# A two-layer decoder step on one core: in the memory layer, weight splits queued behind keys, values and a group norm bias, one head's key transposes in another PSUM pool, and the last head's tail reordered

## The chip, the core and the metric

The kernel runs on one core of a Trainium2 chip. The metric is the device time of one execution in microseconds (us); the runs shown are medians. Engines are named as the profile names them: PE (TensorE matmuls), PEld (its weight loads), DVE (VectorE), ACT (ScalarE), POOL (GpSimd), SP (SyncE, which issues the DMAs).

## The reference: what is computed

One inference step of a two-layer decoder trunk on 320 tokens: 256 of a new prompt and 8 sequences of 8 sampled tokens. Layer 0 mixes tokens with a gated MLP, layer 1 with an mLSTM matrix memory; each is followed by a gated feed-forward layer with a short convolution. The change lies in layer 1, the memory layer. Cut to what matters there:

```
def mlstm_mixer(x, conv_buf, C0, n0, m0, w_in, conv_w, conv_b, b_i, b_f, gn_g, w_out):
    p = x @ w_in                                  # q, k, v, o of 8 heads, gates i, f
    qk, new_buf = causal_dwconv(qk_pre, conv_buf, conv_w, conv_b)
    qk = silu(qk)                                 # q and k: 128 per head; v and o: 256 per head
    h, C, n, m = mlstm_chunkwise(q, k, v32, ig, lf, C0, n0, m0)
    #   scores sc = (q k^T) * w_intra;  num = w_inter * (q C0) + sc v
    #   h = num / max(|den|, exp(-m));  C_new = decay * C0 + (k * g)^T v
    mu, var = mean(h), var(h)                     # group norm over a head's 256
    hn = (h - mu) * rsqrt(var + EPS) * gn_g
    y = (sigmoid(o_pre) * hn) @ w_out
```

All products with weights are float32; every operand is split into a high and a low part, and three matmuls are issued for each pair (high by high, high by low, low by high).

## The kernel before

**Weights.** Every weight block of 128 output columns is read from HBM in chunks of up to 8 tiles of 128x128 (`raw`, four buffers). `weights()` writes the list of all chunks in the order of use (`wq`). `prefetch(n, m)` issues the loads of the first n chunks on SP and the splits of the first m: a cast on ACT (`wh`, L136) and a subtraction on DVE (`wl`, L137), each pair in one of three buffers. `take()` hands out the next chunk, and first has the load of four chunks ahead and the split of one chunk ahead written. `block(kt, rhs)` multiplies a whole block into one of three PSUM banks of the pool `psm` (tile `pm`, 24 matmuls for 8 tiles); all smaller products share the five banks of the pool `psa`.

**Order.** The program is written engine by engine through a scheduling layer: PE's instructions are pinned to the order of the text (`pin`), those of DVE, ACT and POOL may be moved past each other by the layer, and `issue_after(ins)` holds what a block of text writes behind `ins` on that instruction's engine. `behind_split()` uses it to hold the statistics behind the last split. Once built, each engine runs its own list strictly in order.

**The memory layer's loop.** `layer_b` goes over the 8 heads; in the loop body h is the current head, and work of head h-1 is finished inside it. For a head there are six blocks of weights, here called q, k, v0, v1, o0 and o1. Per turn, on PE: block q; `close(h-1)` (the numerators `num` in `numer`, the prompt's new state `pCp` in `state_prompt`); blocks k, v0, v1; `scores(h)` (tiles `pMb`, `psc`); `k_nat(h)` (three transposes of keys into a bank `pk`); `finish(h-1)` (six transposes `phn` of the normed rows `hn`); block o0; `v_nat(h)` (six transposes of values, `pv`); block o1; `hand_over(h)` (`inter`: products of the query with the old state into `num`; `state_sample`: the update `pcs` of the 8 sampled states, in four banks of `psa`; `state_out` adds it to `C` and stores it). For h = 1, `close(0)` and `hand_over(0)` come later, among blocks k, v0 and v1, and `finish(0)` comes after block o0.

**Where the other engines stand.** `qk_epi` turns a block q or k into `qs`: a scaled copy (`bpad`), a convolution of one ACT (`bcv`, L695) and three DVE instructions (L697), a tanh on ACT (`bth`), two products on DVE (`qs`), then the high part on ACT (`qh`, `kh`) and the low part on DVE (`qhl`, `khl`, L281). The third score matmul reads `khl`. `stats(h)` reads `num` on DVE, takes an inverse root on POOL (`sl`, L854), forms the bias `nb` on DVE (L856), and writes `hn` in three ACT instructions (L858), which are the last readers of the three `num` banks. The last turn, h = 7, and what follows the loop mix in blocks of the output weights (`b_wo`): `begin(m)` opens output block m with the rows that are ready, the loop over m at the end closes it with the remaining rows.

Of the kernel before, what the change touches and what calls it, by code (L numbers as in the profile page):

```python
# [10 lines left out]
F32 = mybir.dt.float32  # L11
F32R = mybir.dt.float32r
AF = mybir.ActivationFunctionType
# [3 lines left out]
P = 128  # L17
# [21 lines left out]
class Net:  # L39
# [23 lines left out]
    def weights(self):  # L63
# [32 lines left out]
        add(I["b_wo"], 2, 6, k0=8)  # L96
        add(I["b_wo"], 0, 4, k0=12)
        for b in (1, 2):
            add(I["b_wo"], b, 2, k0=14)
        for b in range(3, KD):  # L100
# [8 lines left out]
    def prefetch(self, n, m):  # L109

        nc = self.nc
        while len(self.loaded) < min(n, len(self.wq)):
            w, b, k0, kn = self.wq[len(self.loaded)]
            raw = self.wraw.tile([P, 8, P], F32, tag="raw", name="raw")
            if w is self.I["a_wv"]:
                kn *= 4
                nc.sync.dma_start(raw[:, :kn, :], w[b, :, 4 * k0:4 * k0 + kn, :])
            else:
                nc.sync.dma_start(raw[:, :kn, :], w[b, :, k0:k0 + kn, :])
            self.loaded.append(raw)  # L120
# [33 lines left out]
    def chunk(self, ps, rhs, first, last):  # L154
        (wh, wl), kn = self.take()
        for k in range(kn):
# [122 lines left out]
    def split(self, yh, yl, y):  # L279
        self.nc.scalar.copy(yh, y)  # L280
        self.nc.vector.tensor_tensor(yl, y, yh.bitcast(F32), op=SUB)  # L281

# [273 lines left out]
    def layer_b(self):  # L556
# [5 lines left out]
        with ExitStack() as ctx:  # L562
# [120 lines left out]
            def qk_epi(h, j, ps):  # L683
# [18 lines left out]
                tv, c_ = [x[:, 256:].rearrange("p (b e) -> p b e", e=11)[:, :, 3:11] for x in (th, cv)]  # L702
                nc.vector.scalar_tensor_tensor(seg(qs[:, TP:T]), tv, 1.0, c_, op0=ADD, op1=MULT)
                nm = "kh" if j else "qh"
# [6 lines left out]
                self.split(hh, ll, qs[:, :n])  # L711
                s["qk"[j]] = (qs, hh, ll)
# [44 lines left out]
            def v_nat(h):  # L757
# [6 lines left out]
                for t in (2, 0, 1):  # L764
                    dst = dsts[t]
                    sc = self.rc[:, t:t + 1] if t < 2 else self.rc2
                    nc.scalar.activation(vh[:, t, :DV], dst[:, :DV], AF.Copy, scale=sc)
                    nc.vector.scalar_tensor_tensor(vl[:, t, :DV], dst[:, :DV], sc, vh[:, t, :DV].bitcast(F32), op0=MULT, op1=SUB)

            def k_nat(h):  # L770
                s = S[h]
                ks = s["k"][0]
                pk = self.psa.tile([P, 512], F32, tag="pa", name="pk")
                for t in range(3):
# [43 lines left out]
            def state_out(h, g):  # L818
                s = S[h]
                dec, C0, pcs = s["P"][2], s["C"][g], s["pcs"][g]  # L820
                for u in range(2):
                    b = 2 * g + u
                    nc.scalar.activation(C0[:, u, :DV], C0[:, u, :DV], AF.Copy, scale=dec[:, b:b + 1])
                nc.vector.tensor_tensor(C0[:, :, :DV], C0[:, :, :DV], pcs.rearrange("p (u v) -> p u v", u=2), op=ADD)
                nc.sync.dma_start(O["Cs"][h, :, 2 * g:2 * g + 2, :], C0[:, :, :DV])
# [15 lines left out]
            def stats(h):  # L841
# [13 lines left out]
                nb = hp.tile([P, 3], F32, tag="nb", name="nb", bufs=1)  # L855
                nc.vector.scalar_tensor_tensor(nb, mv[:, :, 0], -1.0, sl, op0=MULT, op1=MULT)  # L856
                for t in range(3):
# [90 lines left out]
            for h in range(1, NH):  # L948
                last = h == NH - 1
                ps = second if h == 1 else blk()  # L950
                if h > 1:
                    close(h - 1)
# [15 lines left out]
                early(h, 2)  # L968
                ps = blk()
                if h == 1:  # L970
                    with self.behind_split():
                        stats(0)
                v_epi(h, 1, ps)
                scores(h)
                k_nat(h)
                if h > 1:
                    finish(h - 1)
                early(h, 3)
                if last:
                    begin(0)  # L980
                else:
                    o_epi(h, 0, blk())
                if h == 1:
                    finish(0)
                early(h, 4)
                v_nat(h)
                if not last:
                    o_epi(h, 1, blk())
                    hand_over(h)
# [12 lines left out]
            finish(h)  # L1002
            state_sample(h)
            for g in range(4):
                state_out(h, g)
            begin(2)
            nc.gpsimd.tensor_tensor(nS, n0, decs, op=MULT)
            nc.gpsimd.tensor_tensor(nS, nS, nPS[:, :, 2:], op=ADD)
            nc.sync.dma_start(O["nP"], nPS[:, :, 0])
            nc.sync.dma_start(O["nS"], nS)  # L1010
            for m in range(KD):
                ps = part.get(m)
                if ps is None:
                    ps = self.block(8, lambda k: Y[8 + k])
                else:
                    self.chunk(ps, lambda k: Y[done[m] + k], False, True)
                self.residual_norm(m, ps, V_FFN + 8)


# [143 lines left out]
```

## Time and profile before

| | us |
|---|---|
| median of 3 runs (964.19 to 965.17) | 964.74 |
| the profiled execution's own time | 964.48 |
| its span, first to last instruction | 962.8 |
| PE busy | 948.8 (99%) |
| DVE busy | 672.1 (70%) |
| ACT busy | 520.4 (54%) |
| POOL busy | 79.5 (8%) |

The granted TensorE clock is 0.996 over the span. Matmuls are pipelined and their ends are modelled, so PE's gaps are read best as the distance from one matmul's start to the next's: in a block of weights it is 0.15 us, and 24 matmuls take 3.52 us. Timeline rows read: start in us, duration in us, engine, line, operation, out<-in, shapes, count, and in brackets the engine's idle time before the row and what ended it.

The memory layer lies between 425 and 721 us of the span; of its heads, h = 3 takes 514 to 543 us, and the output blocks after the loop start at 692 us.

### The profile page before, as it was taken

Reading aid. Unit: us, or ns where it says so; the run is one execution under the profiler, and the core shown is the slowest. Engines: PE = TensorE matmul, PEld = TensorE weight load, DVE = VectorE, ACT = ScalarE, POOL = GpSimd, SP = SyncE. Lnnn points to the kernel's source line nnn. Section 1 sums busy time; section 2 is a strip of 40 time slices with the busy share of each in tenths; the row PEclk is TensorE's granted clock in tenths of the full one; section 3 lists DMA queues with packets and bytes.
Section 4 is the critical chain, followed back from the end, with each engine's and each line's share of the span. In section 5 each row is a group of like instructions: output and inputs, shape, how many; then the busy total and the mean of one; then the engine's idle time right before and its main releaser. Section 6 shows DMA issues by size and latency. Waiting matters only on the chain.

```text
span 962.8 us, 17155 instructions
## 1 busy us (share of the span) xinstructions
PE 948.8 (99%) x6529; PEld 923.7 (96%) x6529; DVE 672.1 (70%) x1229; ACT 520.4 (54%) x948; POOL 79.5 (8%) x251
## 2 busy tenths in 40 slices
PE   9999999999999999999999999999999999999996
PEld 7779999999999999999899999999999999999996
DVE  5758985577777764549888877676787777775442
ACT  6557444355544543347777776575665555444332
POOL 2200000010000000013211001010101000000000
PEclk9999999999999999999999999999999999999998
DMA  7836344444444454456566555634473444445531
GB/s 252 237 131 183 125 139 150 148 142 154 153 141 152 145 153 151 148 196 209 192 203 203 178 174 187 209 127 152 87 247 136 154 154 150 139 147 153 155 121 55
DMA packets 57560, 154.71 MB, mean 161 GB/s; under 512 B 7734, under 2 KB 19382, under 8 KB 57478
## 3 DMA queue, kind: packets, MB, share of 16 engines
q1 hardware_dynamic: 57478, 153.62, 49.2%
q8 instruction: 51, 0.84, 0.3%
q14 instruction: 31, 0.25, 0.1%
HBM read 141.66 MB, written 11.94 MB: 160 GB/s over the span
## 4 chain that ended last, share of the span: by engine, by line
PE 85%; issue 10%; DVE 2%; DMA 1%; ACT 0%; SPq 0%; POOL 0%; DVEq 0%; POOLq 0%; ACTq 0%
PE pm L48 74%; PE pv L48 3%; PE num L48 2%; DMA raw<-in_a_wv 1%; PE pvs L48 1%; PE pmix L48 1%; DVE wl L137 1%; PE pCp L48 1%; PE psc L48 1%; PE pcs L48 1%; PE pv L51 1%; PE phn L51 0%; PE pk L51 0%; PE pc L48 0%; PE pg L48 0%
## 5 line engine op out<-in xcount | busy, mean ns | idle before, releaser
L136 ACT CAST wh<-raw 128x1024 fp32r<-128x1024 f32 (+3 forms) x255 | 257.9, 1012 | 306.5 <-PE pm L48 167.1
L137 DVE TENSOR_TENSOR wl<-raw,wh 128x1024 fp32r<-128x1024 f32 (+3 forms) x255 | 301.2, 1181 | 137.8 <-ACT wh L136 135.0
L48 PE MATMUL pm<-xh,wh 128*128 128x320 f32 x1216 | 379.7, 312 | 0.0
L48 PE MATMUL pm<-xh,wl 128*128 128x320 f32 x1216 | 376.0, 309 | 0.0
L48 PE MATMUL pm<-xl,wh 128*128 128x320 f32 x1216 | 375.8, 309 | 0.0
L48 PEld LDWEIGHTS pm<-xh,wh 128*128 128x128 f32 x1216 | 228.5, 188 | 0.7
L48 PEld LDWEIGHTS pm<-xl,wh 128*128 128x128 f32 x1216 | 228.5, 188 | 0.2
L48 PEld LDWEIGHTS pm<-xh,wl 128*128 128x128 f32 x1216 | 228.3, 188 | 0.0
L48 PE MATMUL pm<-yh_f,wh 128*128 128x320 f32 x352 | 109.2, 310 | 0.0
L48 PE MATMUL pm<-yh_f,wl 128*128 128x320 f32 x352 | 108.7, 309 | 0.0
L48 PE MATMUL pm<-yl_f,wh 128*128 128x320 f32 x352 | 108.7, 309 | 0.0
L48 PEld LDWEIGHTS pm<-yl_f,wh 128*128 128x128 f32 x352 | 66.1, 188 | 0.0
L48 PEld LDWEIGHTS pm<-yh_f,wh 128*128 128x128 f32 x352 | 66.1, 188 | 0.0
L48 PEld LDWEIGHTS pm<-yh_f,wl 128*128 128x128 f32 x352 | 66.1, 188 | 0.0
L478 DVE SCALAR_TENSOR_TENSOR fcv<-fpad,vecs,fcv 128x336 f32<-128x336 f32 x88 | 49.5, 565 | 2.2 <-ACT fcv L476 0.7
L272 DVE TENSOR_TENSOR xT<-pm,xT 128x320 f32<-128x320 f32 x40 | 19.6, 490 | 42.8 <-PE pm L48 42.8
L48 PE MATMUL pm<-yhb,wh 128*128 128x320 f32 x128 | 40.2, 314 | 0.0
L48 PE MATMUL pm<-yhb,wl 128*128 128x320 f32 x128 | 39.5, 309 | 0.5 <-DVE wl L137 0.5
L48 PE MATMUL pm<-yh_a,wh 128*128 128x320 f32 x128 | 39.6, 309 | 0.0
L48 PE MATMUL pm<-yl_a,wh 128*128 128x320 f32 x128 | 39.5, 309 | 0.0
L48 PE MATMUL pm<-yh_a,wl 128*128 128x320 f32 x128 | 39.5, 309 | 0.0
L48 PE MATMUL pm<-ylb,wh 128*128 128x320 f32 x128 | 39.5, 309 | 0.0
(254 smaller groups left out, 1273.7 us busy)
## 6 DMA issues: line engine op xcount, KB each, us to landing
raw<-in_f_up SPq DMA_DIRECT2D x88, 512.0 KB, 3.3
raw<-in_b_win SPq DMA_DIRECT2D x48, 512.0 KB, 4.4
raw<-in_f_dn SPq DMA_DIRECT2D x32, 448.0 KB, 3.2
C<-in_C SPq DMA_DIRECT2D x32, 258.0 KB, 4.9
raw<-in_a_win SPq DMA_DIRECT2D x16, 512.0 KB, 3.3
raw<-in_a_wo SPq DMA_DIRECT2D x16, 512.0 KB, 3.6
raw<-in_f_dn SPq DMA_DIRECT2D x16, 512.0 KB, 3.5
out_Cs<-C SPq DMA_DIRECT2D x32, 256.0 KB, 4.2
```

The lines of the kernel that those rows point to most:

```text
L48: self.pin(self.nc.tensor.matmul(out, lhsT, rhs, start=start, stop=stop))
L51: self.pin(self.nc.tensor.transpose(out, in_, ident))
L136: self.last_split = nc.scalar.copy(wh[:, :kn, :], raw[:, :kn, :])
L137: self.last_low = nc.vector.tensor_tensor(wl[:, :kn, :], raw[:, :kn, :], wh[:, :kn, :].bitcast(F32), op=SUB)
L272: self.nc.vector.tensor_tensor(x, ps[:, :T], x, op=ADD)
L478: nc.vector.scalar_tensor_tensor(cv, pd[:, i:i + NC], self.vec(w + i * KF), cv, op0=MULT, op1=ADD)
```

## The change

Four things, all in the memory layer:

1. **Splits held back or pulled ahead.** `split`, the convolution's last product, the state's decay, the group norm bias and the value splits are kept by name, and a new helper `behind(...)` holds what is written in its block behind them. For h > 1, the split of the chunk of block o0 is written behind `khl`, and what block v1's `take` writes behind `kh` and `khl`; block o1's `take` is behind the values' halves. `nb` of head h-1 is behind the product `qs` of block k of head h (the name `conv` holds the later of q's and k's). `stats(h-1)` is no longer held behind a split. For h = 1 and h = 2 there are three places more of the kind.
2. **Key transposes of the second head.** For h = 1, `k_nat` writes into a bank of `psm` instead of `psa`.
3. **Order in h = 1.** `finish(0)` comes after `v_nat(1)`, no longer ahead of it.
4. **The tail.** The last rows of output blocks 0, 1 and 2 (4, 2 and 2 tiles) are loaded by three DMAs into one `raw` tile and split at once, not as three chunks. `state_sample(7)` and `state_out(7)` come after output block 2, no longer ahead of `begin(2)`.

```
-        add(I["b_wo"], 0, 4, k0=12)
-        for b in (1, 2):
-            add(I["b_wo"], b, 2, k0=14)
+        q.append((I["b_wo"], ((0, 12, 4), (1, 14, 2), (2, 14, 2)), 0, 8))
...
     def split(self, yh, yl, y):
-        self.nc.scalar.copy(yh, y)
-        self.nc.vector.tensor_tensor(yl, y, yh.bitcast(F32), op=SUB)
+        return (self.nc.scalar.copy(yh, y),
+                self.nc.vector.tensor_tensor(yl, y, yh.bitcast(F32), op=SUB))
+
+    @contextmanager
+    def behind(self, *done):
+
+        with ExitStack() as held:
+            for i in done:
+                held.enter_context(self.tc.issue_after(i.ins))
+            yield
...
-                nc.vector.scalar_tensor_tensor(nb, mv[:, :, 0], -1.0, sl, op0=MULT, op1=MULT)
+                with self.behind(*([S[h + 1]["conv"]] if h + 1 < NH else [])):
+                    s["nb"] = nc.vector.scalar_tensor_tensor(nb, mv[:, :, 0], -1.0, sl, op0=MULT, op1=MULT)
...
-                ps = second if h == 1 else blk()
-                if h > 1:
+                if h == 1:
+                    ps = second
+                else:
+                    with self.behind(*([S[1]["decayed"]] if h == 2 else [])):
+                        ps = blk()
                     close(h - 1)
...
-                ps = blk()
                 if h == 1:
-                    with self.behind_split():
-                        stats(0)
+                    stats(0)
+                else:
+                    with self.behind(S[h]["halves"][1]):
+                        self.prefetch(0, self.used + 2)
+                with self.behind(*S[h]["halves"]):
+                    ps = blk()
                 v_epi(h, 1, ps)
                 scores(h)
-                k_nat(h)
+                k_nat(h, self.psm.tile([P, 512], F32, tag="pm", name="pk") if h == 1 else None)
                 if h > 1:
                     finish(h - 1)
...
-                    o_epi(h, 0, blk())
+                    with self.behind(*([S[0]["nb"]] if h == 1 else [])):
+                        ps = blk()
+                    o_epi(h, 0, ps)
+                if h > 1:
+                    early(h, 4)
+                v_nat(h)
                 if h == 1:
                     finish(0)
-                early(h, 4)
-                v_nat(h)
                 if not last:
-                    o_epi(h, 1, blk())
+                    with self.behind(S[h]["vh"], S[h]["vl"]):
+                        ps = blk()
+                    o_epi(h, 1, ps)
                     hand_over(h)
...
             finish(h)
-            state_sample(h)
-            for g in range(4):
-                state_out(h, g)
             begin(2)
...
+            (wh, wl), k = self.take()
             for m in range(KD):
...
-                    self.chunk(ps, lambda k: Y[done[m] + k], False, True)
+                    n = 16 - done[m]
+                    self.rows(ps, wh, wl, n, lambda k: Y[done[m] + k], False, True)
+                    wh, wl = wh[:, n:, :], wl[:, n:, :]
                 self.residual_norm(m, ps, V_FFN + 8)
+                if m == 2:
+                    state_sample(h)
+                    for g in range(4):
+                        state_out(h, g)
```

`rows` is the loop of `chunk` with the chunk handed in. Up to the memory layer the lists of all engines are the same, and PE's list differs in two places only: in h = 1 the six `pv` stand ahead of the six `phn`, and in the tail the sixteen `pcs` stand 42 matmuls later. On the other engines the built lists show more than the text does. Three places follow.

DVE in the turn h = 3, from the last `rd` of the statistics to the query's `Qz`; before, `wl_6006`, `wl_6099` and `wl_6148` are the low parts of the chunks for o0, o1 and the next head's q, and after, o0's is `wl_6003`.

```order
L852 TENSOR_SCALAR rd_5988<-rd_5988,mv0_4913 128x3
L137 TENSOR_TENSOR wl_6006<-raw_5804,wh_6005 128x1024
L697 TENSOR_SCALAR bcv_5923<-bpad1_4500,vecs_79,bcv_5923 128x344
L856 TENSOR_SCALAR nb_5994<-mv0_4913,sl_5992 128x3
L697 TENSOR_SCALAR bcv_5923<-bpad1_4500,vecs_79,bcv_5923 128x344 x2
L701 TENSOR_SCALAR qs_5930<-bth_5928,bcv_5923 128x256
L703 TENSOR_SCALAR qs_5930<-bth_5928,bcv_5923 128x64
L137 TENSOR_TENSOR wl_6099<-raw_5888,wh_6098 128x1024
L281 TENSOR_TENSOR khl_5934<-qs_5930,kh_5933 128x128
L137 TENSOR_TENSOR wl_6148<-raw_5948,wh_6147 128x1024
L733 TENSOR_SCALAR Qz_4904<-qs_5880,pMb_6036 128x8x8
```

The same place on DVE after:

```order
L860 TENSOR_SCALAR rd_5988<-rd_5988,mv0_4913 128x3
L705 TENSOR_SCALAR bcv_5923<-bpad1_4500,vecs_79,bcv_5923 128x344 x3
L709 TENSOR_SCALAR qs_5930<-bth_5928,bcv_5923 128x256
L711 TENSOR_SCALAR qs_5930<-bth_5928,bcv_5923 128x64
L865 TENSOR_SCALAR nb_5994<-mv0_4913,sl_5992 128x3
L281 TENSOR_TENSOR khl_5934<-qs_5930,kh_5933 128x128
L134 TENSOR_TENSOR wl_6003<-raw_5804,wh_6002 128x1024
L134 TENSOR_TENSOR wl_6099<-raw_5888,wh_6098 128x1024
L741 TENSOR_SCALAR Qz_4904<-qs_5880,pMb_6036 128x8x8
```

No split stands ahead of `khl` any more, `nb` has moved behind `qs`, and the split of the next head's q has left this stretch: it stands after the three `vl`. The turns h = 2 to 6 read alike; in h = 5 and 6, with a block of `b_wo` among them, three splits stand behind `khl`.

ACT in the turn h = 3, from the cast of o0's chunk on, before:

```order
L136 COPY wh_6005<-raw_5804 128x1024
L695 ACTIVATE bcv_5923<-bpad1_4500,vecs_79 128x344
L858 ACTIVATE hn_4906<-num_5842,nb_5994,sl_5992 128x256
L858 ACTIVATE hn_4906<-num_5843,nb_5994,sl_5992 128x256
L858 ACTIVATE hn_4906<-num_5766,nb_5994,sl_5992 128x256
L699 ACTIVATE bth_5928<-bcv_5923 128x344
L716 COPY vTb_5999<-pm_5947 128x256
L717 COPY vTb_5999<-pm_5947 128x128
L136 COPY wh_6098<-raw_5888 128x1024
L710 COPY ks_5935<-qs_5930 128x128
L280 COPY kh_5933<-qs_5930 128x128
```

And after:

```order
L133 COPY wh_6002<-raw_5804 128x1024
L703 ACTIVATE bcv_5923<-bpad1_4500,vecs_79 128x344
L133 COPY wh_6098<-raw_5888 128x1024
L707 ACTIVATE bth_5928<-bcv_5923 128x344
L724 COPY vTb_5999<-pm_5947 128x256
L725 COPY vTb_5999<-pm_5947 128x128
L280 COPY kh_5933<-qs_5930 128x128
L718 COPY ks_5935<-qs_5930 128x128
L867 ACTIVATE hn_4906<-num_5842,nb_5994,sl_5992 128x256
L867 ACTIVATE hn_4906<-num_5843,nb_5994,sl_5992 128x256
L867 ACTIVATE hn_4906<-num_5766,nb_5994,sl_5992 128x256
```

The cast of o1's chunk (`wh_6098`) now stands ahead of the tanh instead of behind the value copies, and the three `hn` stand behind the key's halves instead of ahead of the tanh.

DVE in the tail, from the second of the three small splits (output blocks 0, 1 and 2) to the split of output block 3 (`wl_8315`), before:

```order
L137 TENSOR_TENSOR wl_8274<-raw_8085,wh_8273 128x256
L891 TENSOR_SCALAR y_b_8202<-th_o_8186,phn_8198 128x320
L894 TENSOR_SCALAR ylb_8189<-y_b_8194,gnh_4487,yhb_8188 128x320
L824 TENSOR_TENSOR C0_7847<-C0_7847,pcs_8206 128x2x256
L894 TENSOR_SCALAR ylb_8189<-y_b_8202,gnh_4487,yhb_8188 128x320
L824 TENSOR_TENSOR C0_7849<-C0_7849,pcs_8207 128x2x256
L824 TENSOR_TENSOR C0_7851<-C0_7851,pcs_8208 128x2x256
L824 TENSOR_TENSOR C0_7853<-C0_7853,pcs_8209 128x2x256
L137 TENSOR_TENSOR wl_8297<-raw_8154,wh_8296 128x256
L272 TENSOR_TENSOR xT_76<-pm_8003,xT_76 128x320
L272 TENSOR_TENSOR xT_76<-pm_8037,xT_76 128x320
L137 TENSOR_TENSOR wl_8315<-raw_8243,wh_8314 128x1024
```

And after, where `wl_8240` is output block 3's and `wl_8324` output block 4's:

```order
L134 TENSOR_TENSOR wl_8240<-raw_8087,wh_8239 128x1024
L903 TENSOR_SCALAR ylb_8191<-y_b_8196,gnh_4487,yhb_8190 128x320
L900 TENSOR_SCALAR y_b_8204<-th_o_8188,phn_8200 128x320
L903 TENSOR_SCALAR ylb_8191<-y_b_8204,gnh_4487,yhb_8190 128x320
L134 TENSOR_TENSOR wl_8324<-raw_8156,wh_8323 128x1024
L272 TENSOR_TENSOR xT_76<-pm_8003,xT_76 128x320
L272 TENSOR_TENSOR xT_76<-pm_8037,xT_76 128x320
```

The split of output block 3 has moved from behind the two residual sums `xT` to ahead of the last head's `ylb`, and the four `C` have left this stretch.

More of the change, by code (lines that the diff above doesn't have):

```diff
@@ L114, in prefetch @@
             raw = self.wraw.tile([P, 8, P], F32, tag="raw", name="raw")
[L115 to L119, printed above, removed]
+            e, i = 4 if w is self.I["a_wv"] else 1, 0
+            for b, k0, kn in b if isinstance(b, tuple) else ((b, e * k0, e * kn),):
+                nc.sync.dma_start(raw[:, i:i + kn, :], w[b, :, k0:k0 + kn, :])
+                i += kn
             self.loaded.append(raw)
@@ L155, in chunk, with rows @@
         (wh, wl), kn = self.take()
+        self.rows(ps, wh, wl, kn, rhs, first, last)
+    def rows(self, ps, wh, wl, kn, rhs, first, last):
         for k in range(kn):
@@ L702, in qk_epi @@
                 tv, c_ = [x[:, 256:].rearrange("p (b e) -> p b e", e=11)[:, :, 3:11] for x in (th, cv)]
-                nc.vector.scalar_tensor_tensor(seg(qs[:, TP:T]), tv, 1.0, c_, op0=ADD, op1=MULT)
+                s["conv"] = nc.vector.scalar_tensor_tensor(seg(qs[:, TP:T]), tv, 1.0, c_, op0=ADD, op1=MULT)
                 nm = "kh" if j else "qh"
@@ L710, in qk_epi @@
                     nc.scalar.copy(spread(s["ks"]), twice(qs[:, TP:T]))
-                self.split(hh, ll, qs[:, :n])
+                s["halves"] = self.split(hh, ll, qs[:, :n])
                 s["qk"[j]] = (qs, hh, ll)
@@ L766, in v_nat, with k_nat @@
                     sc = self.rc[:, t:t + 1] if t < 2 else self.rc2
-                    nc.scalar.activation(vh[:, t, :DV], dst[:, :DV], AF.Copy, scale=sc)
-                    nc.vector.scalar_tensor_tensor(vl[:, t, :DV], dst[:, :DV], sc, vh[:, t, :DV].bitcast(F32), op0=MULT, op1=SUB)
-            def k_nat(h):
+                    s["vh"] = nc.scalar.activation(vh[:, t, :DV], dst[:, :DV], AF.Copy, scale=sc)
+                    s["vl"] = nc.vector.scalar_tensor_tensor(vl[:, t, :DV], dst[:, :DV], sc, vh[:, t, :DV].bitcast(F32), op0=MULT, op1=SUB)
+            def k_nat(h, bank=None):
                 s = S[h]
                 ks = s["k"][0]
-                pk = self.psa.tile([P, 512], F32, tag="pa", name="pk")
+                pk = bank or self.psa.tile([P, 512], F32, tag="pa", name="pk")
                 for t in range(3):
@@ L822, in state_out @@
                     b = 2 * g + u
-                    nc.scalar.activation(C0[:, u, :DV], C0[:, u, :DV], AF.Copy, scale=dec[:, b:b + 1])
+                    s["decayed"] = nc.scalar.activation(C0[:, u, :DV], C0[:, u, :DV], AF.Copy, scale=dec[:, b:b + 1])
                 nc.vector.tensor_tensor(C0[:, :, :DV], C0[:, :, :DV], pcs.rearrange("p (u v) -> p u v", u=2), op=ADD)
```

## The prediction

> **What bounds the kernel now.** I read the busy shares on the page first, then a table of two stretches, then PE's waits, and last the timeline around each wait.
>
> ```profile
> span 962.8 us, 17155 instructions
> PE 948.8 (99%) x6529; PEld 923.7 (96%) x6529; DVE 672.1 (70%) x1229; ACT 520.4 (54%) x948; POOL 79.5 (8%) x251
> 502.10:673.10 171.00, 168.52 (x1283) 162.89 (x1282) 134.42 (x288) 112.55 (x258) 16.84 (x42) 1.00 0.53 175
> 703.40:953.00 249.60, 249.60 (x1708) 249.39 (x1707) 161.05 (x258) 115.00 (x184) 13.99 (x70) 1.00 0.44 142
> ```
>
> In the two stretches (length; busy time of PE, PEld, DVE, ACT, POOL; clock) the clock is 1.00. In the last feed-forward layer PE has no gap at all; in the memory layer's heads 2.5 us of 171 are gaps. So PE is the bound, nothing here changes its matmuls, and the change can only win gaps back or open new ones. PE's waits name them:
>
> ```profile
> PE psc L48 <- DVE khl L281: 2.5, 5, 0.5
> PE pk L51 <- ACT hn L858: 1.5, 1, 1.5
> ```
>
> Five times the third score matmul waits for `khl`, once the key transposes wait for `hn`. Here is the former in h = 3, and below it the same pair of matmuls in h = 1, where nothing is waited for.
>
> ```profile
> 530.66 0.28 PE L48 MATMUL psc<-qh,kh 128*128 128x256 f32 x1
> 530.78 0.28 PE L48 MATMUL psc<-qhl,kh 128*128 128x256 f32 x1
> 531.55 0.39 PE L48 MATMUL psc<-qh,khl 128*128 128x256 f32 x1 [0.49 <-DVE khl L281]
> ...
> 532.50 0.38 PE L51 MATMUL phn<-ident,hn 128*128 128x128 f32 x2
> 472.25 0.28 PE L48 MATMUL psc<-qhl,kh 128*128 128x256 f32 x1
> 472.36 0.28 PE L48 MATMUL psc<-qh,khl 128*128 128x256 f32 x1
> ```
>
> From start to start the wait costs 0.77 − 0.11 = 0.66 us, more than the 0.49 in brackets, since the pipeline drains and fills again. All terms below are taken from starts.
>
> **Part 1: the splits, h = 3 to 6.** DVE and ACT of h = 3 before:
>
> ```profile
> 528.70 0.42 DVE L701 SCALAR_TENSOR_TENSOR qs<-bth,bcv 128x256 f32<-128x256 f32 x1 [0.82 <-ACT bth L699]
> 530.07 1.23 DVE L137 TENSOR_TENSOR wl<-raw,wh 128x1024 fp32r<-128x1024 f32 x1 [0.81 <-ACT wh L136]
> 531.22 0.28 DVE L281 TENSOR_TENSOR khl<-qs,kh 128x128 fp32r<-128x128 f32 x1
> 526.81 1.48 ACT L858 ACTIVATE hn<-num,nb,sl 128x256 f32<-128x256 f32 x3 [1.57 <-DVE nb L856]
> 528.17 0.49 ACT L699 ACTIVATE bth<-bcv 128x344 f32<-128x344 f32 x1
> 528.97 1.07 ACT L136 CAST wh<-raw 128x1024 fp32r<-128x1024 f32 x1
> 530.11 0.33 ACT L280 CAST kh<-qs 128x128 fp32r<-128x128 f32 x1
> 519.97 10.69 PE pm L48 x72
> ```
>
> `khl` needs only `kh`, done at 530.44, but a whole split (1.23) stands ahead of it on DVE, whose cast (1.07) stands ahead of `kh` on ACT. Afterwards the split of block o0 is behind `khl`. In exchange the cast for o1 is pulled ahead of `bth`, and it needs the buffer that block v0 has read. The last row, of the chain, gives three blocks (k, v0, v1) from 519.97 to 530.66, 3.56 each; v0 ends at about 527.1. The cast then ends at 527.1 + 1.07 = 528.2, and `bth` at 528.2 + 0.49 = 528.7, against 528.66 before. So `bth` loses nothing, as `hn` (1.48) has left the place ahead of it. From `bth` on `qs`, `kh` and `khl` follow each other: the two `qs` take 0.60 (0.42 and the narrow one), `kh` 0.33 and `khl` 0.28, with hardly a gap 1.2: `khl` is there at about 529.9. Its turn on PE is 530.78 + 0.11 = 530.89. Margin 0.9 to 1.0: the wait goes.
>
> What is late next: `hn`, now behind `kh` on ACT and behind `nb`, which is behind `qs` on DVE. `kh` ends at about 529.6; with the narrow copy behind it `hn`'s 1.48 end at about 531.2. Without the psc wait `phn`'s turn comes at 532.50 − 0.66 = 531.84. Margin 0.6, the thinnest of this change. The split for o0, whose cast stands early on ACT, now follows `khl` on DVE and is needed first by o0's third matmul:
>
> ```profile
> 533.45 0.31 PE L48 MATMUL pm<-xh,wl 128*128 128x320 f32 x1
> ```
>
> at 533.45 − 0.66 = 532.79; an estimate from 529.9 + 1.23 is 531.1, 1.7 early. The split for o1 comes 1.23 behind it, at 532.3, a whole block (3.56) ahead of its use. The next head's q, whose split stood here, goes behind the values' halves; its turn comes only after o1, the `inter` and the update. SP's loads keep their order, four chunks ahead of use, and POOL's list hardly changes; if a load came late, its whole chunk would wait, which the run would show as `pm` waiting. I take the full 0.66 in each of h = 3 to 6: **−2.6**. In h = 2 I take nothing: there the DVE work that h = 1 leaves over reaches into blocks q and k (bounds: −0.66 and, if one split of 1.23 less the 0.49 waited now comes on top, +0.75).
>
> **Part 2 and 3: h = 1.**
>
> ```profile
> 472.71 0.33 PE L48 MATMUL psc<-qs,ks 128*128 128x64 f32 x2
> 474.58 0.44 PE L51 MATMUL pk<-ident,qs 128*128 128x128 f32 x2 [1.54 <-ACT hn L858]
> 473.76 0.16 DVE L856 SCALAR_TENSOR_TENSOR nb<-mv,sl 128x3 f32<-128x3 f32 x1 [0.98 <-POOL sl L854]
> 484.23 0.47 DVE L768 SCALAR_TENSOR_TENSOR vl<-pv,rc,vh 128x256 fp32r<-128x256 f32 x1
> 484.41 0.73 PE L48 MATMUL pcs<-vh,kz 32*128 32x256 f32 x4
> 484.76 0.49 PE L48 MATMUL pcs<-vl,kz 32*128 32x256 f32 x4
> ```
>
> `pk` takes the bank that `hn` reads last: 474.58 − 472.71 less 0.11 is 1.76 lost. In `psm` a bank is free (block v0's, whose last readers are the copies of ACT). But what follows is not free: at the turn's end the update `pcs` already stands 0.35 from its first four to the next ones, waiting for the last `vl`, and that `vl` (and a split, ahead of it) comes at the end of DVE work that is nearly unbroken. PE, arriving 1.76 earlier, waits there longer if that work isn't earlier too. Moving `finish(0)` behind `v_nat(1)` puts one `y_b`, both `ylb` and the split behind the last `vl`, which helps `vl`; but the update also needs the bank that the second `y_b` frees, and the split, of the next turn's block q, is needed 1 us later. I give 0.5 back (a choice: some 0.2 each at the bank and at the split; the bounds are nothing, and all but 0.3): **−1.25**, bounds −0.3 and −1.76.
>
> The last turn of h = 0 has a small one of the kind:
>
> ```profile
> 460.04 1.03 ACT L136 CAST wh<-raw 128x1024 fp32r<-128x1024 f32 x1
> 460.98 0.37 ACT L787 ACTIVATE kgh<-pk,cols 128x128 fp32r<-128x128 f32 x1
> 460.60 0.48 DVE L768 SCALAR_TENSOR_TENSOR vl<-pv,rc,vh 128x256 fp32r<-128x256 f32 x1
> 461.48 0.35 DVE L788 SCALAR_TENSOR_TENSOR kgl<-pk,cols,kgh 128x128 fp32r<-128x128 f32 x1
> 461.88 0.38 PE L48 MATMUL pcs<-vh,kz 32*128 32x256 f32 x1 [0.36 <-DVE kgl L788]
> ```
>
> The fourth `pcs` needs the bank that `kgl` reads last. Without the cast ahead, `kgh` starts at 460.04 and `kgl` directly behind `vl`, at 461.0 instead of 461.48: **−0.49** (least −0.2).
>
> **Part 4: the tail.**
>
> ```profile
> 691.00 0.49 DVE L875 TENSOR_TENSOR o_b<-pm,rb 128x320 f32<-128x320 f32 x1 [2.11 <-PE phn L51]
> 691.48 0.84 PE L48 MATMUL pcs<-vh,kz 32*128 32x256 f32 x4
> 691.94 0.49 PE L48 MATMUL pcs<-vl,kz 32*128 32x256 f32 x4
> 698.59 1.22 DVE L137 TENSOR_TENSOR wl<-raw,wh 128x1024 fp32r<-128x1024 f32 x1
> 699.01 0.31 PE L48 MATMUL pm<-ylb,wh 128*128 128x320 f32 x1
> 699.86 0.41 PE L48 MATMUL pm<-yhb,wl 128*128 128x320 f32 x1 [0.54 <-DVE wl L137]
> ```
>
> The update's second four come 0.46 behind the first, where the steps after cost 0.1 to 0.2, and its first comes late by some 0.1; 42 matmuls (6.2 us) later its operands lie ready for long: −0.4. The split of output block 3 comes late at 699.86, 0.85 behind the matmul before it, less 0.15 is 0.70; with one split instead of three ahead of it, and the update's work between, it is ready: −0.70. On the other side `begin(2)` comes right behind the transposes `phn`, and needs the bank that `o_b` frees at 691.49: +0.15. Sum **−0.95** (bounds −0.3 and −1.15). The merged split is one of 1.22 where three narrower ones stood; it ends on DVE ahead of the transposes' products, while output block 2 has 18 matmuls (2.6 us) to run before its first use, and that hides it. What is late next is the last head's `ylb`, now behind output block 3's split on DVE: about 0.5 of margin by my estimate, so nothing; without that margin it would cost at most the split's 1.22, inside the slow rival's price.
>
> [...] POOL's small product ahead of `nb` lasts either 0.85 or 1.82:
>
> ```profile
> L854 POOL TENSOR_TENSOR sl<-rd,mhalf x8: 848/1825/1830, 472.9 to 685.1; 128x3 f32<-128x3 f32 x8
> ```
>
> The first of the eight, at 472.9, runs while DVE idles ahead of `nb` and ends 0.9 us later, so it is the short one; the usual one is longer by 0.98. [...]
>
> **The sum.** −0.49 − 1.25 − 2.6 − 0.95 = −5.3. Against the profiled execution (964.48: span 962.8 and 1.68 around it) that gives 959.2; the median 964.74 is 0.26 above it, and 964.74 − 5.3 = **959.4**.
>
> **The rivals.**
>
> *The backlog stays (22%).* The same mechanism, only with less room: after h = 1 DVE is behind by more than I think; the 1.25 is given back at `pcs`, and the first two of the four waits stay. For it: the unbroken DVE work from 478.68. Against: h = 3 to 6 have slack on DVE (134.4 of 171 busy). Gain 5.3 − 1.25 − 1.3 = 2.8: 961.9.
>
> *The waits only change name (10%).* `phn` waits for `hn` where `psc` waited for `khl`: if `hn` comes 1.26 later than I work out (0.6 margin and 0.66), part 1 is nothing; with the tail given back as well, −0.49 − 1.25 = −1.8 stays, 963.0. For it: `nb` and `hn` are now the last of the chain. Against: the whole of `hn` is only 1.48.
>
> *Slower: `hn` becomes the bound (10%).* With one more cast between `qs` and `hn` on ACT (1.07: a cast that waits for its buffer holds the tanh and all behind it) and `sl` in its long case (1.82 − 0.85 = 0.98 more) the rows come 2.05 later than I have them. Less the margin 0.6 that is 1.45 at `phn` per head; in the six heads h = 2 to 7 it is 8.7, and with the gains of 5.3 the time is 3.4 above: 968.1. It decides from about 1.5 us per head, where 6 × 0.9 eats the whole gain. Against: the list of before already has o0's cast ahead of the tanh, and in h = 3 `sl` has long ended when `qs` lets `nb` go.
>
> **How the numbers follow.** My forecast has 58%, its own range 957.4 (largest gains: 0.49 + 1.76 + 3.3 + 1.15 = 6.7, and the `pcs` gap and the scatter of the runs) to 961.0 (the low ends of h = 0, h = 1 and the tail). 959.4 is its middle case. With the backlog and half the renaming rival the range is **957.4 to 963.4**; above it lie the slow rival and a tail of the other, some 15%, and below it a few per cent. The low end of every term at once, 0.2 + 0.3 + 0.3 and two of the four waits, is 2.1, which lies inside it. A measurement of this kernel tells about 0.2%, 1.9 us, from no change: faster means below 962.8, slower above 966.7. Faster is my forecast, the backlog and a sliver of the renaming, 0.82; the same 0.08; slower 0.10.
>
> **What would show it.** In the profile afterwards: PE's waits of `psc` for `khl` gone in h = 3 to 6, the third matmul 0.11 behind the second; `pk` of h = 1 directly behind `psc`; no 0.54 wait for `wl` in the tail. My steps are wrong if PE waits for `hn` at `phn`, if `pcs` in h = 1 stands longer than 0.35 behind its first four by more than 0.5, or if `psc` of h = 2 waits over 0.75 longer. All is wrong if blocks of weights themselves wait for `wl`.

## The result and the profile after

The changed kernel takes 957.10 us (median of 6 runs, 956.81 to 957.26), against 964.74 before (964.12 to 965.66): a ratio of 0.9921, interval 0.9910 to 0.9932, 7.6 us less. The forecast was 959.4 with a range from 957.4; the sign was right, and the time lies 0.3 below the range. Two points of the section on the change have to be put right: only `stats(0)` lost its hold behind a split, for the later heads that hold stayed; and what block v1's `take` writes is held behind `kh` and `khl` in h = 1 too, not only for h > 1.

The page after, and a stretch of heads 2 to 6 that holds the same 1,283 matmuls as the one shown of before (columns as there: length; busy time of PE, PEld, DVE, ACT, POOL; clock, DMA share, GB/s):

```profile
span 955.4 us, 17155 instructions
PE 946.2 (99%) x6529; PEld 921.9 (96%) x6529; DVE 669.0 (70%) x1227; ACT 519.2 (54%) x946; POOL 76.6 (8%) x251
499.54:666.74 167.20, 167.20 (x1283) 162.58 (x1282) 132.98 (x288) 112.68 (x260) 12.49 (x42) 1.00 0.55 180
```

The stretch is 167.2 us instead of 171.0, and PE has no gap left in it. All of PE's waits that the view lists for the whole profile are now these, none in the memory layer:

```profile
PE pw L48 <- DVE ones L1064: 1.2, 1, 1.2
PE pv L48 <- ACT wh L133: 0.4, 1, 0.4
PE pc L48 <- ACT sq L192: 0.3, 1, 0.3
```

The turn h = 3 on PE, DVE and ACT:

```profile
527.45 0.28 PE L48 MATMUL psc<-qhl,kh 128*128 128x256 f32 x1
527.57 0.28 PE L48 MATMUL psc<-qh,khl 128*128 128x256 f32 x1
...
528.09 0.39 PE L51 MATMUL pk<-ident,qs 128*128 128x128 f32 x2
...
528.42 0.38 PE L51 MATMUL phn<-ident,hn 128*128 128x128 f32 x2
525.99 0.29 DVE L281 TENSOR_TENSOR khl<-qs,kh 128x128 fp32r<-128x128 f32 x1 [0.15 <-ACT kh L280]
526.20 2.35 DVE L134 TENSOR_TENSOR wl<-raw,wh 128x1024 fp32r<-128x1024 f32 x2
526.06 1.47 ACT L867 ACTIVATE hn<-num,nb,sl 128x256 f32<-128x256 f32 x3
```

`khl` ends at 526.28, 1.29 us before the matmul that reads it; `hn` ends at 527.53, 0.89 before the first transposition. In h = 1 and at the end of its turn:

```profile
472.22 0.33 PE L48 MATMUL psc<-qs,ks 128*128 128x64 f32 x2
472.39 0.39 PE L51 MATMUL pk<-ident,qs 128*128 128x128 f32 x2
480.41 0.48 DVE L776 SCALAR_TENSOR_TENSOR vl<-pv,rc,vh 128x256 fp32r<-128x256 f32 x1
481.26 0.48 DVE L900 SCALAR_TENSOR_TENSOR y_b<-th_o,phn 128x320 f32<-128x320 f32 x1
482.17 0.39 PE L48 MATMUL pcs<-vh,kz 32*128 32x256 f32 x4
482.39 0.29 PE L48 MATMUL pcs<-vl,kz 32*128 32x256 f32 x4
```

The transposes follow `psc` directly, the last `vl` ends 1.3 us before the update, and the old gap inside the update (0.35) has gone too: its second four come 0.22 behind the first.

In h = 2 the third score matmul waited like those of h = 3 to 6, and no longer does (first row before, second row after):

```profile
502.95 0.38 PE L48 MATMUL psc<-qh,khl 128*128 128x256 f32 x1 [0.51 <-DVE khl L281]
499.72 0.28 PE L48 MATMUL psc<-qh,khl 128*128 128x256 f32 x1
```

To see where the time went, both profiles' PE instructions were put side by side, and at each the distance of the two start times was taken; where it changes, time was won or lost. Below this is called "by starts". (us; the first layer, where the program is the same, differs by 0.17, scatter.)

| place | forecast | measured |
|---|---|---|
| h = 0, fourth bank of the update | −0.49 | −0.33 |
| h = 1, transposes and update | −1.25 | −2.06 (−1.74 and −0.32) |
| h = 2 | 0 | −0.77 |
| h = 3 to 6 | −2.6 | −3.01 (4 times −0.75) |
| tail | −0.95 | −0.97 |
| memory layer | −5.3 | −7.1 |

### The profile page after: what moved, and what is told of

The parts are those of the page before. It is cut to its first block, busy times and chain, and to the rows that moved or that the text cites. A ratio compares the mean times of both kernels' runs of the same rounds, so it can differ in the third digit from the quotient of the medians.

```text
span 955.4 us, 17155 instructions
## 1 busy us (share of the span) xinstructions
PE 946.2 (99%) x6529; PEld 921.9 (96%) x6529; DVE 669.0 (70%) x1227; ACT 519.2 (54%) x946; POOL 76.6 (8%) x251
## 4 chain that ended last, share of the span: by engine, by line
PE 89%; issue 9%; DMA 0%; DVE 0%; SPq 0%; DVEq 0%; ACT 0%; POOLq 0%; POOL 0%
PE pm L48 76%; PE pv L48 5%; PE num L48 2%; PE pvs L48 2%; PE pmix L48 1%; PE pCp L48 1%; PE psc L48 1%; PE pcs L48 1%; PE pv L51 1%; PE phn L51 0%; DMA raw<-in_a_wv 0%; PE pk L51 0%; PE pc L48 0%; PE pg L48 0%; PE pb L48 0%
## 5 line engine op out<-in xcount | busy, mean ns | idle before, releaser
L133 ACT CAST wh<-raw 128x1024 fp32r<-128x1024 f32 (+2 forms) x253 | 256.7, 1018 | 302.0 <-PE pm L48 163.9
L134 DVE TENSOR_TENSOR wl<-raw,wh 128x1024 fp32r<-128x1024 f32 (+2 forms) x253 | 298.9, 1186 | 133.5 <-ACT wh L133 131.2
```

The costliest lines, as they stand in the source:

```text
L133: self.last_split = nc.scalar.copy(wh[:, :kn, :], raw[:, :kn, :])
L134: self.last_low = nc.vector.tensor_tensor(wl[:, :kn, :], raw[:, :kn, :], wh[:, :kn, :].bitcast(F32), op=SUB)
```

## The experiments

All times are medians beside runs of the kernel before on the same chip; its median was 964.3 to 964.6 in the four groups. Effects below 1 us are read from the profile by the same comparison of starts, since the first layer alone, where all programs are the same, differs by up to 0.6 from one profile to another.

**The bank alone.** On the kernel before:

```
-                k_nat(h)
+                k_nat(h, self.psm.tile([P, 512], F32, tag="pm", name="pk") if h == 1 else None)
```

> The kernel before with one edit: the key transposes of h = 1 in a bank of psm. Theory P (the forecast's): the wait of 1.74 us at the transposes goes, but the update at the turn's end then waits for vl and the fifth bank, and gives a part back: 0.3 to 1.25 us faster, 963.5 to 964.4. Theory W (every wait simply goes): 1.74 faster, 963.0, and the gap of 0.33 in the update stays as it is.

Measured: 965.46 against 964.59, ratio 1.0006 (0.9997 to 1.0015); no gain. The profile shows −1.70 at the transposes and +1.59 at the update:

```profile
PE pcs L48 <- DVE vl L768: 1.5, 1, 1.5
483.32 0.39 PE L48 MATMUL pcs<-vh,kz 32*128 32x256 f32 x3
485.24 0.38 PE L48 MATMUL pcs<-vh,kz 32*128 32x256 f32 x1 [1.54 <-DVE vl L768]
487.00:490.30 3.30, 3.30 (x15) 3.30 (x14) 1.71 (x3) 0.70 (x2) 0.00 (x0) 0.50 0.88 247
```

The last row is a stretch 1.8 us behind that wait: the granted clock is 0.50 for 3.3 us, and the block running there takes 1.54 longer. So theory P was right in kind and too mild: in this profile the bank, alone, gives back nearly its whole gain, and more where the clock falls.

**The bank and PE's order.** The edit before, and `finish(0)` moved behind `v_nat(1)`.

> The kernel before with two edits: the key transposes of h = 1 in a bank of psm, and finish(0) behind v_nat(1). Theory O (the order is what keeps the gain): the last vl no longer stands behind y_b and both ylb, the update waits less, and most of the 1.74 us stays: 1.2 to 2.0 faster than before, 962.7 to 963.5, and no stretch at half clock. Theory H (the holds of the change are needed as well): a split and the y_b still stand ahead of the last vl, the update waits 0.5 to 1.5 again: 0 to 1 faster.

Measured: 963.59 against 964.39, ratio 0.9991 (0.9981 to 1.0000), clock 1.00. At the transposes −1.70, at the update of h = 1 +0.41 (it waits for both `y_b` and then for the last `vl`, which stands behind them), in h = 2 +0.32 (the first score matmul waits for `kh`, the third for `khl`), and at the update of h = 7 +0.36 (it waits for `y_b`). Both theories are half right: most of the wait's return is gone, and a part stays.

**With two holds in h = 1.** In addition:

```
+                    with self.behind(*([S[0]["nb"]] if h == 1 else [])):
+                        ps = blk()
...
+                    with self.behind(*([S[h]["vh"], S[h]["vl"]] if h == 1 else [])):
+                        ps = blk()
```

> The kernel before with the bank, finish(0) behind v_nat(1), and in h = 1 two holds: the split from block o0's take behind nb of head 0, that from block o1's take behind vh and vl. Theory H (the two splits ahead of the last vl cost the rest): the update of h = 1 no longer waits, nor does it have its old gap of 0.33: 2.0 faster than before at that place instead of 1.3, 962.6. Theory X (a split that is held then comes too late for the block that needs it): 0.2 to 1 us of waits for wl at o1 or at the next q, and the time stays at 963.3 or above.

Measured: 963.62 against 964.45, ratio 0.9989 (0.9979 to 0.9998), no better than without. But the place moved: the update now has no wait and lost its old gap (−1.70 and −0.33, as in the changed kernel), and h = 2 pays for it with 0.32 + 0.68 + 0.17 = 1.17 us. The profile's row of the first score matmul there:

```profile
501.11 0.39 PE L48 MATMUL psc<-qh,kh 128*128 128x256 f32 x1 [0.52 <-ACT kh L280]
```

It is theory X in kind, at another place. Two splits (2.35 us) now run on DVE from 484.32 on, inside block q of h = 2, and the four `C` and the epilogue of that block stand behind them. That this makes the key of h = 2 late is read from the order; no run tests it apart.

**The splits' order alone.** On the kernel before, for h > 1:

```
-                ps = blk()
+                    with self.behind(S[h]["halves"][1]):
+                        self.prefetch(0, self.used + 2)
+                    with self.behind(*S[h]["halves"]):
+                        ps = blk()
```

> The kernel before with one edit: for h > 1 the splits that take() writes for block v1 and for o0 are held behind the key's halves; the norm's bias nb stays where it was, so the three hn still stand ahead of the tanh on ACT, now with a cast behind them. Theory K (the place of khl alone is the cause): the wait at the third score matmul goes in all of h = 2 to 6, 0.75 each, 3.8 us faster, 961.0. Theory N (moving hn is needed too): the chain hn 1.48, cast 1.07, tanh, qs, kh, khl ends at 530.9 in h = 3, just at the turn of 530.9, so that part of the wait stays, 0.1 to 0.4 per head, and the gain is 2 to 3 us.

Measured: 961.17 against 964.59, ratio 0.9965 (0.9952 to 0.9978), 3.4 less; by starts −0.77 in h = 2 and −0.75 in each of h = 3 to 6. Theory K. In h = 3 `khl` is there 1.1 us early although `hn` still stands ahead of the tanh on ACT:

```profile
525.16 1.47 ACT L866 ACTIVATE hn<-num,nb,sl 128x256 f32<-128x256 f32 x3 [0.60 <-DVE nb L864]
527.46 0.50 ACT L707 ACTIVATE bth<-bcv 128x344 f32<-128x344 f32 x1
528.79 0.29 DVE L281 TENSOR_TENSOR khl<-qs,kh 128x128 fp32r<-128x128 f32 x1 [0.23 <-ACT kh L280]
530.22 0.28 PE L48 MATMUL psc<-qh,khl 128*128 128x256 f32 x1
```

My chain for theory N took `hn` at its old time; with no split ahead of `nb` on DVE, `nb` and `hn` come about 1 us earlier against PE's turn.

**Each hold taken out of the changed kernel, and both.** The edits: the lines just shown taken out, for all h; or `nb` written without `behind(... ["conv"])`; or both.

> The changed kernel without one edit: the splits for blocks v1 and o0 are held behind nothing, for all h; nb stays behind qs. Theory K: a split stands ahead of khl again, the third score matmul waits in h = 2 to 6, +3.8 us, and with h = 0's cast ahead of kgh again +0.5: 961.4. Theory N: hn behind kh alone frees the tanh by its 1.48 us, the waits return by less than half, +1 to +2, 958 to 959.

> The changed kernel without one edit: nb is not held behind qs, so that hn may stand ahead of the tanh on ACT again. Theory K: khl has 1.3 us to spare in h = 3 (its end 526.28, the matmul's turn 527.57) and stays in time in most heads: within 0.4 us of the changed kernel, 957.1 to 957.5. Theory N: hn's 1.48 go ahead of the tanh, khl is late by 0.2 to 0.4 in five heads, +1 to +2, 958 to 959.

> The changed kernel without both holds of the splits behind the key's halves and of nb behind qs. Either hold alone kept h = 3 to 6 free of waits. Theory R (the two are redundant there): without both, the third score matmul waits 0.75 in h = 3 to 6 again, and h = 0 and h = 2 lose what they lost without the splits' holds: +3.0 + 1.9 = 4.9, 962.0. Theory V (what frees h = 3 to 6 is that the next block q's split has left the place behind the values): the waits stay away, 958.9 as without the splits' holds.

Measured: 958.94, 958.38 and 961.44 us. By starts, against the changed kernel:

| | h = 0 | h = 2 | h = 3 to 6 | h = 7 |
|---|---|---|---|---|
| without the splits' hold | +0.36 | +1.25 | 0 | +0.64 |
| without the hold of `nb` | 0 | +0.99 | 0 | 0 |
| without both | +0.34 | +1.27 | 4 times +0.77 | 0 |

In h = 3 to 6 either hold is enough, and without both the old wait is back in full:

```profile
PE psc L48 <- DVE khl L281: 2.3, 5, 0.5
```

That is theory R. With one hold out, the times lie where theory N had them, but the place is another: nothing in h = 3 to 6, all of it in h = 2 and at the edges (in h = 7 the numerators wait 0.6 for `vl`). So N's range was met by luck; K was wrong on the first and on the second kernel by 2.5 and 0.9. Without the splits' hold a split does stand ahead of the key, but with `hn` gone from ACT its cast is earlier, and it runs while DVE has nothing to do but wait for the tanh (kernel without the splits' hold, DVE):

```profile
526.09 1.23 DVE L134 TENSOR_TENSOR wl<-raw,wh 128x1024 fp32r<-128x1024 f32 x1 [0.55 <-ACT wh L133]
527.24 0.42 DVE L709 SCALAR_TENSOR_TENSOR qs<-bth,bcv 128x256 f32<-128x256 f32 x1
528.02 0.29 DVE L281 TENSOR_TENSOR khl<-qs,kh 128x128 fp32r<-128x128 f32 x1 [0.16 <-ACT kh L280]
```

There PE reads `khl` at 528.85. In h = 2 both holds are needed; that the splits left over from h = 1 are the reason is again read from the order.

**Bank and order taken out of the changed kernel.** Two kernels: the key transposes of h = 1 in `psa` again; or `finish(0)` ahead of `v_nat(1)` again.

> The changed kernel with the key transposes of h = 1 in psa again. Theory W (waits simply add): the transposes wait for hn, which ends at 474.93, from 472.39 on: 2.5 us, of which the gap in the update gives nothing back: 957.1 + 2.5 = 959.6. Theory P (DVE's work behind sets the end of that turn): part of the wait is taken up by slack on PE's side at the update, +1 to +1.8: 958.1 to 958.9.

> The changed kernel with the old order of PE in h = 1: finish(0) ahead of v_nat(1) and early. Theory O: the vl stand behind y_b and ylb again, the update of h = 1 waits 1 to 1.6 us as it did with the bank alone, and if the clock falls to half behind that wait, up to 1.5 more: 958.1 to 960. Theory H: with the splits held back the vl come in time: within 0.4 of the changed kernel.

Measured: 958.62 and 958.27. Without the bank the transposes wait 1.72 for `hn`, and by starts nothing of it is given back later. The time lies in theory P's range by luck: the mechanism is W's with a shorter wait than I put: the bank is free once the first of the three `hn` has read it, at 472.95 + 0.56 = 473.51 in this kernel's profile.

```profile
472.95 1.48 ACT L867 ACTIVATE hn<-num,nb,sl 128x256 f32<-128x256 f32 x3 [1.22 <-DVE nb L865]
473.57 0.44 PE L51 MATMUL pk<-ident,qs 128*128 128x128 f32 x2 [1.55 <-ACT hn L867]
```

With the old order the update takes 0.70 more and the next block q waits 0.72 for its split: +1.4, with the clock at 1.00; theory O.

**Two smaller holds.** The split behind `vh` and `vl`, in all heads; and the two further holds around h = 1 and 2.

> The changed kernel without one edit: the split that block o1's take() writes (the next turn's block q) is not held behind vh and vl. Theory H (this hold brings the vl of h = 1 in time): the update of h = 1 waits 0.4 to 1 us for vl or y_b, and in h = 2 to 6 nothing: 957.5 to 958.1. Theory D (the split comes ahead of Qz and of the value halves in all heads and makes the updates late): 0.3 or more in each of six heads, 959 or more. Theory Z: no matter, within 0.2.

> The changed kernel without the two further holds around h = 1 and 2: block o0's take behind nb of head 0, and block q's take of h = 2 behind the state's decay. Theory H: one of them keeps a split from standing ahead of nb and the vl of h = 1; without them the update of h = 1 or the blocks behind wait 0.4 to 1.5 us: 957.5 to 958.6. Theory Z: no matter, within 0.2.

Measured: 957.37 and 957.68. By starts +0.24 and +0.10; the rest of these medians is the first layer's scatter. The 0.24 lies at the update of h = 1, which again waits for the last `vl`: theory H's place, at less than its size. The 0.10 lies in block q of h = 2. Each alone is worth little.

**The tail.** The changed kernel with the update ahead of `begin(2)` again; and with three chunks and three splits again.

> The changed kernel with the last head's update and its stores ahead of begin(2) again; the merged split stays. Theory A (the terms add): the gap of 0.4 in the update comes back and begin(2) loses its wait of 0.15: +0.25, 957.4. Theory B (the four C also go back ahead of output block 3's split on DVE): the wait for wl comes back as well, +0.9 to 1.0, 958.1.

> The changed kernel with the last rows of output blocks 0, 1 and 2 as three chunks with three splits again; the update stays behind block 2. Theory A: the split of output block 3 comes behind the xT sums again and late, +0.7, 957.8. Theory B: with the update behind block 2 PE has 1.3 us more ahead of block 3's second pass, and the split is in time: within 0.2.

Measured: 957.28 and 961.58. The first is theory A, +0.18 by starts. The second is neither: with the update moved but the splits not merged, block 3's split is in time, as theory B has it, but PE waits 3.3 us at the third matmul of output block 4 for that block's split, and the clock falls to 0.51 behind it.

```profile
PE pm L48 <- DVE wl L136: 3.3, 1, 3.3
696.67 1.28 DVE L834 TENSOR_TENSOR C<-C,pcs 128x512 f32<-128x512 f32 x2
697.87 1.22 DVE L136 TENSOR_TENSOR wl<-raw,wh 128x1024 fp32r<-128x1024 f32 x1
699.14 0.41 PE L48 MATMUL pm<-yhb,wl 128*128 128x320 f32 x1 [3.32 <-DVE wl L136]
700.50:703.50 3.00, 3.00 (x13) 3.00 (x12) 2.12 (x4) 0.00 (x0) 0.00 (x0) 0.51 0.78 258
```

The four `C`, moved with the update, stand ahead of that split on DVE. With the merged split it comes ahead of them, at 689.22 in the changed kernel, where the `C` start at 694.08. So the move needs the merged split; the merged split without the move loses only 0.18.

**Extra copies ahead of `hn`.** To make `hn` late, 4 or 7 copies were added ahead of the three `hn` of each head of the changed kernel; nothing is left out:

```
+                for _ in range(4):
+                    nc.scalar.activation(hn[:, 0, :], num[0][:, :DV], AF.Identity, scale=sl[:, 0:1], bias=nb[:, 0:1])
```

> The changed kernel with four extra copies of the first hn tile written ahead of the three hn in every head, 0.46 us each on ACT, 1.84 in all; nothing is left out. It puts hn late on purpose, as the slow rival had it. Theory M (hn has a margin of 1.1 us in h = 3 to 7 and 0.5 in h = 2, its end against the third transposition's turn, and past it PE pays in full): 1.3 + 5 x 0.74 = 5.0 slower than the changed kernel, 962.1. Theory F (the forecast's margin of 0.6 in all six): 6 x 1.24 = 7.4, 964.5. Theory S (something behind takes the wait up): under 3.

> The changed kernel with seven such copies, 3.2 us in all, so that PE stands for about 2 us at the transposes of each head, as it did once at the update with the bank alone, where the clock fell to half behind it. Theory G (a gap of about 2 us can bring the clock down to half for some 3 us, 1.5 us each time): 13.3 us for the waits (2.7 + 5 x 2.1) and 1.5 for each head in which the clock falls, 970 to 980, and stretches of 0.5 in the granted clock behind the waits. Theory C (the fall was the doing of that place, not of the gap): clock 1.00 throughout, 970.4.

Measured: 969.32 and 999.12. With four copies PE stands 1.42 longer at `phn` in h = 2 and in each of h = 3 to 6, and 1.21 in h = 7; the turn h = 1 takes 1.5 more and the last head's `begin(2)` 1.2, two places that no theory had. It is 12.2 in all, over every theory. In h = 3:

```profile
532.19 0.59 ACT L869 ACTIVATE hn<-num,nb,sl 128x256 f32<-128x256 f32 x1
...
531.30 0.27 PE L51 MATMUL pk<-ident,ks 128*128 128x128 f32 x1
532.83 0.44 PE L51 MATMUL phn<-ident,hn 128*128 128x128 f32 x2 [1.26 <-ACT decs L739]
```

The last `hn` ends at 532.78, and the first transposition starts 0.05 later: it waits for all three, where theory M let two go ahead (the row names `decs`, the next one on ACT; `hn` is what it reads). And two copies of values slipped in between, so `hn` was 2.31 late, not 1.84. 2.31 − 0.89 (the margin shown above) is the 1.42: past its margin PE pays in full. With seven copies PE stands 2.85 to 3.85 us at each of eight places, and at seven of them the clock falls: theory G in kind, but 42 us slower than the changed kernel where its range ended at 23; the hardware's part is below.

## Why the prediction was wrong, point by point

- **PE is the bound and only gaps can be won.** Right: in the heads' stretch 171.0 became 167.2 with the same matmuls. The steps that failed are the next three.
- **h = 3 to 6.** The mechanism was right (`khl` ahead of the split, in time by 1.29 where I had 0.9 to 1.0), and the size too small: −0.75 each, not −0.66. I measured the wait to the start of the matmul that waited. The group from its first matmul to the transposes took 1.51 before (530.66 to 532.17) and 0.75 after (527.34 to 528.09): 0.1 more is lost behind the wait, while the pipeline fills: the next matmul starts 0.22 behind the one that waited, and 0.12 where nothing waited. I had written that sentence and cut the interval one matmul too early. Missed: 0.4 us.
- **h = 2.** "I take nothing" was wrong: −0.77. The late key there had the same cause as in the other heads (it is one of the five waits of the view in the prediction); the splits' order alone, on the kernel before, removes it. The work left over from h = 1 that I feared is there, but the change's holds deal with it: the kernel with the bank, the order and h = 1's holds alone pays 1.17 there, and the changed kernel without either of the holds in h = 2 pays 1.0 to 1.3. Missed: 0.8 us.
- **h = 1.** "I give 0.5 back" failed too: −2.06, not −1.25. The mechanism I named exists: the bank alone gives back 1.59 of 1.70. With PE's order it is 1.29 that stays, near my number; but with the two holds of that turn nothing is given back, and the old gap of 0.33 in the update, which I had left standing, goes too (−1.70 and −0.33 in the kernel with the bank, the order and these holds). The hold behind the values alone brings 0.24 at that place in the changed kernel. I had one split behind the last `vl`, but put it down to the moved `finish(0)`, and still took off 0.2 for the bank and 0.2 for that split; neither cost anything. Missed: 0.8 us.
- **h = 0 and the tail.** −0.33 for −0.49: `kgl` did come directly behind `vl`, only that `vl` ends later than the start I gave `kgl` (by the row shown, 460.60 + 0.48 = 461.08, not 461.0). The hold brings it: without the splits' hold 0.36 comes back. The tail's −0.97 was −0.95, partly by luck: the split brought 0.8 where I had 0.70, the moved update 0.18 where I had 0.25. That the move without the merged split loses 4.5 us I did not see.
- **The rivals.** The backlog came true in kernels with a part of the change, not in the whole. That waits only change name: `hn` has 0.89 us to spare instead of 0.6. The slow rival did not happen. Its rule for the price was right: `hn` 2.31 late cost 1.42 per head, which is the lateness less the real margin of 0.89. With its margin of 0.6 it was too dear per head, but it left out the turn h = 1 and `begin(2)` (1.5 and 1.2 at that lateness), and the clock when `hn` is later still.
- **The range.** Its low end took the largest gain of three terms, but for h = 2 to 6 only −3.3, five times the cut interval. With 0.75 it would have reached 956.95, and held the time. The three misses add up: 0.8 + 0.8 + 0.4 = 2.0, of which h = 0 takes 0.16 back; 5.3 + 1.8 = 7.1, and the first layer's scatter in the two profiles makes it 7.3 by starts, near their spans' difference of 7.4. The medians differ by 7.64, since the one before lies 0.26 above its profiled execution.

## What to carry to other kernels

A wait that you remove can come back at the next place where the same engine's work is due: cost the built order of the whole turn, all holds together, not each edit by itself. Here the bank alone won nothing, two holds were redundant in four heads and both needed in one, and moving the update without merging the splits would have lost 4.5 us. Measure a wait from the first instruction of its group to the first behind it that is not affected; and when a bound is left at nothing because "a backlog may reach there", look in the lists of after for what works it off.

## What the runs showed of the hardware

**The granted clock fell behind some gaps on PE, not at once and not always.** Distances on PE from start to start, in the kernels of this case: ten of 1.32 to 1.83 us had a clock of 1.00 behind them; of ten others, at one of 1.92 and eight of 2.85 to 3.85 the clock fell to 0.50, for 3.41 or 6.83 us by the trace's record of the clock; at one of 3.85 it did not. After the one of 1.92 the fall came about 1.8 us later, when PE was busy again; at four of those of 3.85 it came 1.2 to 1.6 us before PE went on. Two gaps of equal length in the kernel with seven copies, with the stretch behind each:

```profile
508.03:514.80 6.77, 6.77 (x30) 6.77 (x31) 3.40 (x9) 2.75 (x8) 0.00 (x0) 0.59 0.02 7
662.20:668.00 5.80, 5.80 (x41) 5.80 (x42) 5.32 (x12) 3.36 (x9) 0.00 (x0) 1.00 0.01 6
```

In that kernel the seven falls begin 27.3, 34.1, 34.1, 41.0, 88.7 and 20.5 us after one another: 8, 10, 10, 12, 26 and 6 times 3.41 us, the length of the shorter falls. Why one of two equal gaps brought a fall and the other did not, no run shows. The runs with the bank alone lie in two groups, four of 963.7 to 964.4 with a mean clock of 0.996 to 0.998 and six of 965.4 to 966.5 with 0.995 or 0.996, as if the clock fell in six of ten; only one of them has a profile.

**POOL's `sl` takes 0.85 in all eight heads after**, where it took 1.83 in five of eight before. In those five a split of 1.26 us on DVE ran beside its start; after, no split runs beside any of the eight. Other DVE work does:

```profile
L862 POOL TENSOR_TENSOR sl<-rd,mhalf x8: 848/850/863, 472.4 to 678.8; 128x3 f32<-128x3 f32 x8
497.68 0.85 POOL L862 TENSOR_TENSOR sl<-rd,mhalf 128x3 f32<-128x3 f32 x1
497.93 0.42 DVE L709 SCALAR_TENSOR_TENSOR qs<-bth,bcv 128x256 f32<-128x256 f32 x1 [0.49 <-ACT bth L707]
```

So beside the start of a split `sl` took 0.98 longer, five times of five, and beside the product of the keys it did not: in h = 2 that product started while `sl` ran, and neither took longer than elsewhere (0.42 us, its usual length, and 0.85). In h = 3 to 7 the convolution's products (0.58, usually 0.57) ran beside `sl` in the same way.
